# Reordering the opening of a two-layer decoder kernel: one table first, four PSUM banks for the input's transposes, dummies in a bank of their own, the first weights in four transfers

## The chip, the cores and the metric

One core of a Trainium2 chip runs the whole kernel. The metric is the device time of one execution in microseconds (us), the median of several runs.

## The reference

A decoder trunk of two layers on 256 tokens of width 1024, float32. Each layer is a mixer and a mixture of experts, each with a residual and a layer norm. The opening concerns the first lines alone: the input's layer norm and the mixer's one combined projection.

```python
h = layer_norm(x, ln_in_g, ln_in_b)
for l in range(2):
    # inside mixer_block: split_cols(h @ w_in[l], IN_SPLITS) feeds three attention mixers and three gates
    mix = mixer_block(h, l, w_in[l], ...)
    h = layer_norm(DEEPNORM_ALPHA * h + mix, ln1_g[l], ln1_b[l])
    ffn = moe_ffn(h, router_w, router_b, moe_w1[l], moe_w3[l], moe_w2[l])
    h = layer_norm(DEEPNORM_ALPHA * h + ffn, ln2_g[l], ln2_b[l])
```

## The kernel before

**Precision.** A projection is computed from operands split in two: a high half rounded to fp32r and a low half that holds the rest. One product is three matmuls (high by high, low by high, high by low). ScalarE casts the high half of a weight block (L370, or L949 for the first one), VectorE subtracts to get the low half (L371, L950). Each block is 128 partitions by 2048 columns, 1 MB, split 1024 columns at a time.

**Weights** come through a ring of SBUF slots (`Stream`, L81 to L136). A load is issued on SP as soon as a slot is free, in a fixed order: "q" 0 and 1 (the query columns), "kv" 0 and 1, "ng", and so on. The block ("q", 0) is loaded in two transfers (L98), every other in one.

**The opening** (L186 to L217, L1681 to L1699). ScalarE's queue issues the identity (`idf`, from `consts`) and then the per-column constants (`pc`). SP issues x, one transfer for each half of 128 tokens, and then the weights. While the data comes, TensorE runs three dummy matmuls on a tile of ones (`junk`, L1688), into a buffer of the same PSUM pool that the transposes use. `raw_T` (L287) transposes x, eight column tiles by two token halves (L291). A tile of 128 x 256 takes one of four PSUM buffers. `raw_split` (L294) multiplies it by the norm's gain: ScalarE writes the high half (`z`, L297), VectorE the low half (L298), and then the buffer is free for the tile four places on.

**The raw products.** The query projection does not wait for the layer norm. Block ("q", 0) (L964) and block ("q", 1) (L375 to L377, from `z`) are multiplied with the raw, transposed x, 48 matmuls each, and corrected afterwards with the tokens' scale and shift (L977 to L980). The first block is split in two halves of four tiles: the first by L949 and L950 (`gl`), the second by `split` (L370, L371). The load of the norm's gain and bias rows (`gb`, L216) is issued on ScalarE's queue behind the cast of L949.

**The norm.** `norm` (L922) computes statistics of each token half (L310), aggregates them (L254), takes a reciprocal root by three steps of Newton's method (L235 to L242), the shift (L260), and normalizes x in place: VectorE does the first 512 columns (L271), ScalarE the others (L267). TensorE transposes the result (L319), ScalarE applies gain and bias (L337), VectorE splits it (L338, L339), and the "kv" projection is the first product with the normalized input (`acc<-hi,whi`, L375). Layer 1 does the same with values that the experts' stage left, through the same lines, except that x is there already transposed and its statistics are read in PSUM (L935).

**What sets the order.** The kernel is written in one order. A scheduler turns it into one instruction stream for each engine, by a list of ready instructions, priorities and its own estimates of time. `tc.issue_after(i)` holds an instruction behind `i` on the same engine. Each engine runs its stream in that order. The same program gives each DMA one of eight completion counters in turn.

Of the kernel before, what the change touches and what calls it, by code (L numbers as in the profile page):

```python
# [9 lines left out]
F32 = mybir.dt.float32  # L10
# [4 lines left out]
ALU = mybir.AluOpType  # L15
AX = mybir.AxisListType
PSUM = bass.MemoryType.PSUM

L = 2
P = 128  # L20
D = 1024
S = 256
KD = D // P
# [13 lines left out]
LOANS = (6, 7)  # L37
NW = 16
NW2 = 24
NW0 = 3  # L40
NS = NA + 3 + NB + 2 + NC + 1
EARLY = set()
DOWN = [[], [0], [1], [2, 3], [], [4], [5], [6, 7]]
# [8 lines left out]
CB_SEL = CB_IOTA + 64  # L52
CB_LOW = CB_SEL + 2
CB_TRI = CB_LOW + 16
CB_ID = CB_TRI + P
CB_N = CB_ID + 3 * P

PC_LN = 0
PC_QG = 80
# [3 lines left out]
PC_N = PC_POS + 64  # L63
# [6 lines left out]
def trunk(ctx, tc, x, consts, pcol, rowv, gb, wfm, wng, wdv, wmla, wcmp, wcmp2, wu, wbr, wout, rw, mw1, mw3, mw2, out):  # L70
    import numpy as np
    nc = tc.nc
    slopes = [float(v) for v in _slopes(np)]
    V, A, T, G = nc.vector, nc.scalar, nc.tensor, nc.gpsimd

    cst = ctx.enter_context(tc.tile_pool(name="cst", bufs=1))
# [4 lines left out]
    class Stream:  # L81
# [6 lines left out]
        def load(self, slots, item):  # L88
            slot = slots.pop(0)
            key, src, n = item  # L90
            t = slot[0].tile([P, 2048], F32, name="wt", tag=slot[1])
            eng = nc.sync
            if key[1:] == ("w2", 15, 1):
                for c in (0, 256):
                    d, v = [a.rearrange("p (b c) -> p b c", c=512)[:, :, c:c + 256] for a in (t, src)]
                    eng.dma_start(d, v)
            else:
                parts = 2 if key[1:] == ("q", 0) else 1  # L98
                for c in range(0, n, n // parts):
                    eng.dma_start(t[:, c:c + n // parts], src[:, c:c + n // parts])  # L100
            self.live[key] = (t, slot, slots)
# [83 lines left out]

    rt = hp.tile([P, 2, D], F32, name="r")  # L186
    idb = cst.tile([P, 3 * P], F32R, name="idb")
    pc = cst.tile([P, PC_N], F32, name="pc")
    start = ExitStack()
    gi = start.enter_context(tc.tile_pool(name="gi", bufs=1, reuse_waits="tile"))  # L190
    ident = gi.tile([P, P], F32, name="idf")
    nc.scalar.dma_start(ident, consts[:, CB_ID + P:CB_ID + 2 * P])
    nc.scalar.dma_start(pc, pcol)
    for t in range(2):
        nc.sync.dma_start(rt[:, t], x[t * P:(t + 1) * P, :])
    ST.pump()
# [66 lines left out]
    def ln_norm2(r, sts, src=None):  # L263
        mr, nbs, _ = ln_mr2(sts)
        for t in range(2):
            d = r[:, t, 512:1024]
            A.activation(d, d if src is None else src[t][1], AF.Identity, bias=nbs[t], scale=mr[t][1])  # L267
        for q in range(2):
            for t in range(2):
                d = r[:, t, 256 * q:256 * q + 256]  # L270
                i = V.tensor_scalar(d, d if src is None else src[t][0][:, 256 * q:256 * q + 256], mr[t][0], mr[t][1],  # L271
                                    op0=ALU.subtract, op1=ALU.mult)
        return [rs for mu, rs in mr], nbs, i.ins
# [10 lines left out]
            z += [(zt[:, k, 0], zt[:, k, 1]) for k in range(n)]  # L284
        return z

    def raw_T(r, i, ks, z, psp):  # L287
        for k in ks:
            ps = psp.tile([P, S], F32, name="pt")
            for t in range(2):  # L290
                T.transpose(ps[:, t * P:(t + 1) * P], r[:, t, k * P:(k + 1) * P], ident)  # L291
            raw_split(ps, i, k, z)

    def raw_split(ps, i, k, z):  # L294
        g = ln_cols(i, k)[0]
        hi, lo = [v[:, 0:S] for v in z[k]]
        X0["z", k] = A.activation(hi, ps, AF.Copy, scale=g).ins  # L297
        V.scalar_tensor_tensor(lo, ps, g, hi.bitcast(F32), op0=ALU.mult, op1=ALU.subtract)  # L298

    def raw_fix(rs, nbs, psp, bc):  # L300
        ps = psp.tile([P, 2, S], F32, name="s")
# [5 lines left out]
    def ln_stats(r, t):  # L307
        st = sm.tile([P, 2, 6], F32, name="lnst")
        for c in range(2):
            V.bn_stats(st[:, c], r[:, t, c * 512:(c + 1) * 512])  # L310
        return st
# [31 lines left out]
    def mixer(l, res, z, zf):  # L343
# [578 lines left out]
        def norm():  # L922
            r, i = res, 2 * l
            pool, tag = ST.take()
            if zf is None:
                rs, nbs, X["norm"] = ln_norm2(r, [ln_stats(r, t) for t in range(2)])
            else:
                zt = [[p.tile([P, 512], F32, name=n) for c in range(2)] for p, n in ((pO, "o"), (pS, "s"))]
                sts = [sm.tile([P, 2, 6], F32, name="lnst") for t in range(2)]
                for c in range(2):  # L930
                    for t in range(2):
                        for k in range(4):
                            with tc.issue_after(X["raw", 0, 0]):
                                T.transpose(zt[t][c][:, k * P:k * P + P], zf[:, 4 * c + k, t * P:t * P + P], ident)
                        V.bn_stats(sts[t][:, c], zt[t][c])  # L935
                rs, nbs, X["norm"] = ln_norm2(r, sts, zt)
            bc = pool.tile([P, 2048], F32, name="bc", tag=tag)
            psps = [(pT, "pt"), (pT, "pt"), (pO, "o"), (pO, "o"), (pS, "s")]
            xT[:] = ln_split_T(r, i, X["evq"], psps, *(ST.take() if zf is None else X0["zf"]))
            with tc.issue_after(X["evq"]):  # L940
                raw_fix(rs, nbs, pS, bc)
            return bc
# [2 lines left out]
        add_tm("ng", xT, 280, ev2)  # L945
        w = wtile("q", 0, KD, 256)
        gl = mg.tile([P, 2, 4, 256], F32R, name="gl", tag="gt0")
        with tc.issue_after(X0["z", 1 if "yh" in X0 else 3]):
            i = A.copy(gl[:, 0], w[:, 0:4])  # L949
        V.tensor_sub(gl[:, 1], w[:, 0:4], gl[:, 0].bitcast(F32))  # L950
        with tc.issue_after(i.ins):
            w0 = [(gl[:, 0], gl[:, 1]), split(w[:, 4:8], [P, 4, 256], mb, OHL[1][1])]
        with tc.issue_after(i.ins):
            for c in fq[2:4]:
# [724 lines left out]
        return r, Z.get("z"), Z.get("zf")  # L1679

    with start as st:  # L1681
        pi = st.enter_context(tc.tile_pool(name="pi", bufs=4, space=PSUM))
        A.activation(one, one, AF.Identity)
        junk = gi.tile([P, 4 * P], F32, name="junk")
        V.memset(junk, 1.0)
        pj = pi.tile([P, S], F32, name="pt")
        for _ in range(NW0):
            T.matmul(pj, junk[:, 0:P], junk[:, 0:S], start=True, stop=True)  # L1688
        trf = gi.tile([P, P], F32, name="trf")
        zero = gi.tile([P, P], F32, name="zero")  # L1690
        G.memset(zero, 0.0)
        for j, v in enumerate((zero, ident, zero)):
            G.tensor_copy(idb[:, j * P:j * P + P], v)
        nc.sync.dma_start(trf, consts[:, CB_TRI:CB_ID])
        V.tensor_copy(tri, trf)
        z = raw_tiles(0)
        raw_T(rt, 0, range(KD), z, pi)
        ident = idb[:, P:2 * P].bitcast(F32)

    zf = None  # L1700
# [8 lines left out]
def _consts(np):  # L1709
# [21 lines left out]
    ang = np.arange(256, dtype=f)[:, None] * freqs[None, :]  # L1731
    c[:, CB_COS:CB_COS + 32] = np.cos(ang).astype(f).reshape(2, P, 16).transpose(1, 0, 2).reshape(P, 32)
    c[:, CB_SIN:CB_SIN + 32] = np.sin(ang).astype(f).reshape(2, P, 16).transpose(1, 0, 2).reshape(P, 32)
    c[:, CB_ID + P:CB_ID + 2 * P] = np.eye(P, dtype=f)
    c[:, CB_TRI:CB_TRI + P] = (np.arange(P)[:, None] < np.arange(P)[None, :])
    c[:, CB_IOTA:CB_IOTA + 64] = np.arange(1, 65)[None, :]
    c[:, CB_LOW:CB_LOW + 16] = (np.arange(4)[:, None] > np.arange(4)[None, :]).astype(f).reshape(1, 16)
# [4 lines left out]
def _pack(np, inp):  # L1742
# [61 lines left out]
    for l in range(L):  # L1804
        for n in ("cmp_pos_k", "cmp_pos_v"):
            pcs.append(a[n][l].reshape(16, 2, 64).transpose(1, 2, 0).reshape(P, 16))
    pcol = np.concatenate(pcs, 1)
    rowv = np.concatenate([a["router_b"]] + [a["diff_lambda"][l].reshape(-1) for l in range(L)])
    return {
        "x": a["x"].reshape(S, D), "consts": _consts(np), "pcol": pcol, "rowv": rowv, "gb": gb, "wfm": wfm, "wng": wng, "wdv": wdv,  # L1810
# [20 lines left out]
```

## Time and profile before

| | us |
|---|---|
| median of 3 runs | 1046.31 |
| the runs | 1044.56 to 1046.35 |
| the profiled execution | 1044.16 |
| its span, first to last instruction | 1042.5 |

The profiled execution is one execution by itself. Its span is a little shorter than its time, which also holds what lies before the first instruction and after the last. PE is TensorE's matmul part, PEld its weight load, DVE is VectorE, ACT ScalarE, POOL GpSimd; a q behind an engine's name (ACTq, SPq) is its queue, where it issues DMAs. Busy times say what an engine did, waits what it stood for: an idle stretch is put down to what ended it. The times in a timeline count from the first instruction.

### The profile page before, as it was taken

To read this page: it belongs to the slowest core of one execution; us is meant where nothing else is said; L and a number is where in the kernel's file an instruction comes from. 1 tells how busy PE (TensorE), PEld (TensorE's weight loads), DVE (VectorE), ACT (ScalarE), POOL (GpSimd) and SP (SyncE) were. 2 spreads that over 40 slices of the span, in tenths; PEclk is the share of its full clock that TensorE was granted. 3 is DMA by queue.
4 is the path that set the end of the run, shared out by engine and by line. 5 is a ranking of instruction groups with operands and counts; after the bars stand their busy time and mean duration, and the time that the engine had idled before them with its cause. 6 is when DMAs were issued, how large, how long until landed. Compare 5 with 4: busy or idle time off the path is not lost. (4 is left out here: it accounts for less than half of the span.)

```text
span 1042.5 us, 16792 instructions
## 1 busy us (share of the span) xinstructions
PE 1005.7 (96%) x6498; PEld 707.3 (68%) x6498; DVE 533.7 (51%) x1493; ACT 423.7 (41%) x991; POOL 31.7 (3%) x46
## 2 busy tenths in 40 slices
PE   8999999999989999999899999999999999989994
PEld 7888888999864344433597888799998544424332
DVE  7755778785772121211395558777777422102315
ACT  6564677564432121211455547755553221101110
POOL 0300000000000000000001001000000000000001
PEclk8999999999999999999999999999999999999998
DMA  9664334548867999999955544345497789999993
GB/s 358 250 243 137 138 122 164 182 141 345 321 258 302 422 420 420 420 421 420 389 182 215 188 152 155 130 146 177 158 374 300 290 321 422 421 418 421 420 421 133
DMA packets 45543, 294.88 MB, mean 283 GB/s; under 512 B 5136, under 2 KB 7952, under 8 KB 11792
## 3 DMA queue, kind: packets, MB, share of 16 engines
q1 hardware_dynamic: 44880, 291.51, 71.3%
q10 hardware_dynamic: 576, 2.24, 0.5%
q8 instruction: 51, 0.84, 0.3%
q14 instruction: 36, 0.29, 0.1%
HBM read 292.68 MB, written 1.05 MB: 282 GB/s over the span
## 5 line engine op out<-in xcount | busy, mean ns | idle before, releaser
L1557 PE MATMUL pt<-wt,xe 128*64 128x512 f32 x1024 | 226.3, 598 | 5.3 <-DVEq L1453 4.7
L371 DVE TENSOR_TENSOR wlo<-wt,whi 128x1024 fp32r<-128x1024 f32 (+4 forms) x146 | 167.4, 1148 | 81.9 <-ACT whi L370 75.7
L370 ACT CAST whi<-wt 128x1024 fp32r<-128x1024 f32 (+4 forms) x146 | 143.8, 987 | 147.1 <-PE acc L376 103.5
L1557 PEld LDWEIGHTS pt<-wt,xe 128*64 128x64 f32 x1024 | 72.9, 138 | 143.9 <-issue 133.7
L375 PE MATMUL acc<-hi,whi 128*128 128x256 f32 x576 | 165.4, 289 | 1.7 <-ACT whi L370 0.8
L377 PE MATMUL acc<-hi,wlo 128*128 128x256 f32 x576 | 164.0, 286 | 0.8 <-DVE wlo L371 0.8
L376 PE MATMUL acc<-lo,whi 128*128 128x256 f32 x576 | 162.3, 282 | 0.0
L1600 PE MATMUL pt<-wt,gT 128*64 128x512 f32 (+1 forms) x544 | 113.9, 568 | 0.0
L375 PEld LDWEIGHTS acc<-hi,whi 128*128 128x128 f32 x576 | 108.1, 188 | 7.9 <-issue 3.9
L377 PEld LDWEIGHTS acc<-hi,wlo 128*128 128x128 f32 x576 | 108.3, 188 | 4.2 <-DVE wlo L371 2.1
L376 PEld LDWEIGHTS acc<-lo,whi 128*128 128x128 f32 x576 | 108.7, 189 | 0.3 <-DVE lo L339 0.2
L1609 ACT CAST yh<-pt 128x512 fp32r<-128x512 f32 (+1 forms) x34 | 19.1, 560 | 184.2 <-PE pt L1600 184.2
L1600 PEld LDWEIGHTS pt<-wt,gT 128*64 128x64 f32 x544 | 38.7, 137 | 70.6 <-issue 65.8
L1610 DVE TENSOR_TENSOR yl<-pt,yh 128x512 fp32r<-128x512 f32 (+1 forms) x34 | 22.4, 659 | 106.0 <-ACT yh L1609 106.0
L1568 DVE SCALAR_TENSOR_TENSOR g<-g,pt 128x512 f32<-128x512 f32 x16 | 11.0, 686 | 126.6 <-ACT g L1567 126.6
L1567 ACT ACTIVATE g<-pt 128x512 f32<-128x512 f32 x16 | 9.6, 597 | 120.4 <-PE pt L1557 120.4
L375 PE MATMUL acc<-ob,whi 128*128 128x256 f32 x192 | 56.8, 296 | 1.1 <-DVE gt L892 0.8
L376 PE MATMUL acc<-ob,whi 128*128 128x256 f32 x192 | 54.2, 282 | 0.0
L377 PE MATMUL acc<-ob,wlo 128*128 128x256 f32 x192 | 54.2, 284 | 0.0
L1569 DVE SCALAR_TENSOR_TENSOR g<-g,wsl,pt 128x512 f32<-128x512 f32 x16 | 11.9, 746 | 69.0 <-PE pt L1557 69.0
L659 DVE COPY ts<-pt 128x384 f32<-128x384 f32 x56 | 30.5, 551 | 30.7 <-PE pt L628 30.6
L1382 ACT ACTIVATE xe<-pt,pc 128x128 f32<-128x128 f32 x60 | 24.2, 453 | 53.3 <-PE pt L1324 51.6
(399 smaller groups left out, 1763.1 us busy)
## 6 DMA issues: line engine op xcount, KB each, us to landing
wt<-in_mw SPq DMA_DIRECT2D x190, 1024.0 KB, 16.8
wt<-in_wfm SPq DMA_DIRECT2D x38, 1024.0 KB, 4.9
wt<-in_wbr SPq DMA_DIRECT2D x12, 1024.0 KB, 4.8
wt<-in_wcmp SPq DMA_DIRECT2D x8, 1024.0 KB, 6.2
wt<-in_wout SPq DMA_DIRECT2D x8, 1024.0 KB, 8.1
wt<-in_wdv SPq DMA_DIRECT2D x4, 1024.0 KB, 6.2
wt<-in_wmla SPq DMA_DIRECT2D x4, 832.0 KB, 5.8
wt<-in_wng SPq DMA_DIRECT2D x4, 560.0 KB, 12.8
```

The source lines that it names most:

```text
L370: X["hi"] = A.copy(hi, src).ins
L371: X["lo"] = V.tensor_sub(lo, src, hi.bitcast(F32)).ins
L375: T.matmul(ps, a[0], b[0], start=start, stop=False)
L376: T.matmul(ps, a[0], b[1], start=False, stop=False)
L377: return T.matmul(ps, a[1], b[0], start=False, stop=stop)
L659: X["ts"] = V.tensor_copy(ts, pt).ins
L1382: A.activation(x[:, k], pj, AF.Identity, bias=bb, scale=g)
L1557: i = T.matmul(hh[64 * j:64 * j + 64], xe[p][:, 2 * h + k, j * CAP:(j + 1) * CAP], wt[:, c0:c0 + FF], start=(h == 0 and k == 0), stop=(h = ...
L1569: V.scalar_tensor_tensor(g, g, wsl[:, p:p + 1], h3, op0=ALU.mult, op1=ALU.mult)
L1600: i = T.matmul(v[64 * j:64 * j + 64], gT[:, 2 * h + f, 64 * j:64 * j + 64], w2t[:, c0 + ks[0] * P:c0 + ks[1] * P], start=(h == 0 and f == ...
L1609: X0["yh"] = A.copy(yh[:, d], v).ins
L1610: V.tensor_sub(yl[:, d], v, yh[:, d].bitcast(F32))
```

## The change

- The identity is put ahead of the per-column constants in one table (`pct`), loaded in one transfer on ScalarE's queue ahead of all else. It leaves `consts`.
- The block ("q", 0) of layer 0 comes in four transfers, that of layer 1 in two as before.
- The transposes of x go into four tiles of a whole PSUM bank, two column tiles in each. All of the first token half come first, then all of the second, in an order written out. ScalarE's eight high halves are chained one behind another.
- The dummies go into a bank of their own: four ahead of the transposes, and three behind them.
- The cast of the first half of the first block (`gl`) is done in two pieces, behind the second and the fourth tile of `z` in layer 0; the other half's cast follows the last tile there.
- In layer 0 VectorE's statistics of the second token half follow the last low half of `z`, and the aggregation and normalization follow the low halves of the second block.
- The cast of the triangular mask (`tri`) goes from VectorE to GpSimd.

```diff
-NW0 = 3
+NW0 = 4
+NW1 = 3
...
-                parts = 2 if key[1:] == ("q", 0) else 1
+                parts = (4 if key[0] == 0 else 2) if key[1:] == ("q", 0) else 1
...
-    pc = cst.tile([P, PC_N], F32, name="pc")
+    pct = cst.tile([P, P + PC_N], F32, name="pc")
+    ident, pc = pct[:, 0:P], pct[:, P:]
...
-    ident = gi.tile([P, P], F32, name="idf")
-    nc.scalar.dma_start(ident, consts[:, CB_ID + P:CB_ID + 2 * P])
-    nc.scalar.dma_start(pc, pcol)
+    nc.scalar.dma_start(pct, pcol)
...
-    def raw_T(r, i, ks, z, psp):
-        for k in ks:
-            ps = psp.tile([P, S], F32, name="pt")
-            for t in range(2):
-                T.transpose(ps[:, t * P:(t + 1) * P], r[:, t, k * P:(k + 1) * P], ident)
-            raw_split(ps, i, k, z)
+    def raw_T(r, i, z, psp, fill):
+        ps = [psp.tile([P, 2, S], F32, name="pt") for k in range(KD // 2)]
+        ps = [v[:, k] for k in range(2) for v in ps]
+        for t in range(2):
+            for k in range(KD):
+                with tc.issue_after(fill):
+                    fill = T.transpose(ps[k][:, t * P:(t + 1) * P], r[:, t, k * P:(k + 1) * P], ident).ins
+        for k in range(KD):
+            with tc.issue_after(X0["z", k - 1]) if k else nullcontext():
+                raw_split(ps[k], i, k, z)
+        return fill
...
-        V.scalar_tensor_tensor(lo, ps, g, hi.bitcast(F32), op0=ALU.mult, op1=ALU.subtract)
+        X0["zl", k] = V.scalar_tensor_tensor(lo, ps, g, hi.bitcast(F32), op0=ALU.mult, op1=ALU.subtract).ins
...
-                rs, nbs, X["norm"] = ln_norm2(r, [ln_stats(r, t) for t in range(2)])
+                sts = [ln_stats(r, 0)]
+                with tc.issue_after(X0["zl", 7]):
+                    sts.append(ln_stats(r, 1))
+                with tc.issue_after(X["lo"]):
+                    rs, nbs, X["norm"] = ln_norm2(r, sts)
...
-        with tc.issue_after(X0["z", 1 if "yh" in X0 else 3]):
-            i = A.copy(gl[:, 0], w[:, 0:4])
-        V.tensor_sub(gl[:, 1], w[:, 0:4], gl[:, 0].bitcast(F32))
-        with tc.issue_after(i.ins):
+        for n, k in enumerate((1, 1) if "yh" in X0 else (1, 3)):
+            v = slice(2 * n, 2 * n + 2)
+            with tc.issue_after(X0["z", k]):
+                i = A.copy(gl[:, 0, v], w[:, v])
+            V.tensor_sub(gl[:, 1, v], w[:, v], gl[:, 0, v].bitcast(F32))
+        with tc.issue_after(i.ins if zf is not None else X0["z", 7]):
             w0 = [(gl[:, 0], gl[:, 1]), split(w[:, 4:8], [P, 4, 256], mb, OHL[1][1])]
...
-        pi = st.enter_context(tc.tile_pool(name="pi", bufs=4, space=PSUM))
+        pi = st.enter_context(tc.tile_pool(name="pi", bufs=4, space=PSUM, reuse_waits="tile"))
...
-        pj = pi.tile([P, S], F32, name="pt")
-        for _ in range(NW0):
-            T.matmul(pj, junk[:, 0:P], junk[:, 0:S], start=True, stop=True)
+        pjp = st.enter_context(tc.tile_pool(name="pj", bufs=1, space=PSUM, reuse_waits="tile"))
+        pj = pjp.tile([P, S], F32, name="pj")
+
+        def fill(n):
+            for _ in range(n):
+                i = T.matmul(pj, junk[:, 0:P], junk[:, 0:S], start=True, stop=True)
+            return i.ins
+        warmed = fill(NW0)
...
-        V.tensor_copy(tri, trf)
+        G.tensor_copy(tri, trf)
         z = raw_tiles(0)
-        raw_T(rt, 0, range(KD), z, pi)
+        with tc.issue_after(raw_T(rt, 0, z, pi, warmed)):
+            X0["fill"] = fill(NW1)
```

## Rows read from the trace of the kernel before

**Rows 1.** The page's first line.
```profile
span 1042.5 us, 16792 instructions
```

**Rows 2.** Busy time by stretch: us, PE, PEld, DVE, ACT, POOL, granted clock, DMA share, GB/s.
```profile
6.00:8.60 2.60, 0.65 (x4) 0.42 (x4) 2.53 (x13) 1.57 (x4) 0.00 (x0) 1.00 0.86 285
8.97:15.70 6.73, 6.45 (x30) 5.89 (x29) 6.67 (x20) 5.56 (x8) 0.00 (x0) 0.50 1.02 432
...
20.00:1040.00 1020.00, 990.42 (x6425) 694.59 (x6424) 518.24 (x1446) 412.47 (x973) 30.50 (x38) 0.99 0.72 282
```

**Rows 3.** Waits of the whole kernel: us in total, times, longest us.
```profile
PE pt L1557 <- DVEq L1453: 4.7, 1, 4.7
PEld pt L1600 <- DMA wt<-in_mw: 2.0, 5, 0.8
```

**Rows 4.** Timeline of PE in the opening: start us, us, what, idle before.
```profile
1.71 2.93 PE L1688 MATMUL pt<-junk 128*128 128x256 f32 x6 [1.71 <-DVE junk L1685]
5.12 0.83 PE L291 MATMUL pt<-idf,r 128*128 128x128 f32 x4 [0.48 <-DMA idf<-in_consts]
6.37 0.65 PE L291 MATMUL pt<-idf,r 128*128 128x128 f32 x4 [0.42 <-DMA r<-in_x]
8.66 1.28 PE L291 MATMUL pt<-idf,r 128*128 128x128 f32 x4 [1.64 <-DVE z L298]
10.10 2.52 PE L964 MATMUL acc<-z,gl 128*128 128x258 f32 x10 [0.15 <-ACT gl L949]
...
18.00 1.12 PE L964 MATMUL acc<-z,wlo 128*128 128x258 f32 x8
...
27.92 0.28 PE L375 MATMUL acc<-hi,whi 128*128 128x256 f32 x1
```

**Rows 5.** Timeline of ScalarE and its queue in the opening.
```profile
6.74 1.57 ACT L297 ACTIVATE z<-pt,pc 128x256 fp32r<-128x256 f32 x4 [3.47 <-PE pt L291]
9.00 1.04 ACT L949 CAST gl<-wt 128x1024 fp32r<-128x1024 f32 x1 [0.70 <-DMA wt<-in_wfm]
10.29 0.34 ACTq L216 DMA_DIRECT2D gb<-in_gb  x1
10.67 0.47 ACT L297 ACTIVATE z<-pt,pc 128x256 fp32r<-128x256 f32 x1 [0.62 <-DMA wt<-in_wfm]
```

**Rows 6.** DMA issues of the first 40 us: KB each, median us to landing.
```profile
pc<-in_pcol ACTq DMA_DIRECT2D x1, 76.0 KB, 5.3
idf<-in_consts ACTq DMA_DIRECT2D x1, 64.0 KB, 4.2
```

**Rows 7.** Groups of VectorE from 4.8 to 29.7 us: busy us, mean ns, idle before.
```profile
L371 DVE TENSOR_TENSOR wlo<-wt,whi 128x1024 fp32r<-128x1024 f32 x7 | 8.6, 1222 | 2.6 <-ACT whi L370 2.5
...
L310 DVE BATCH_NORM_STATS2 lnst<-r 128x6 f32<-128x512 f32 x4 | 2.6, 682 | 3.2 <-DMA r<-in_x 3.2
```

**Rows 8.** Timelines of VectorE and PE in layer 1's norm.
```profile
528.86 0.32 DVE L254 BATCH_NORM_AGGREGATE lnmv<-lnst 128x2 f32<-128x12 f32 x2
529.33 1.22 DVE L371 TENSOR_TENSOR wlo<-wt,whi 128x1024 fp32r<-128x1024 f32 x1
533.13 0.99 DVE L271 TENSOR_SCALAR r<-s,lnmv,rqy 128x256 f32<-128x256 f32 x2
535.53 0.38 PE L319 MATMUL pt<-idb,r 128*128 128x128 f32 x2
538.23 0.50 PE L375 MATMUL acc<-hi,whi 128*128 128x256 f32 x2
```

**Rows 9.** The mask's readers: duration ns min, median, max, first and last start.
```profile
L1215 PEld LDWEIGHTS <-tri x2: 102/142/181, 294.7 to 300.5; 128*128 128x128 bf16 x2
```

**Rows 10.** Timeline of VectorE in the opening: a step of the norm and a low half.
```profile
15.07 0.21 DVE L240 SCALAR_TENSOR_TENSOR rqt<-rqy,rqh 128x1 f32<-128x1 f32 x1
15.20 1.22 DVE L371 TENSOR_TENSOR wlo<-wt,whi 128x1024 fp32r<-128x1024 f32 x1
```

**Rows 11.** Timeline of SP's queue.
```profile
9.00 0.33 SPq L200 DMA_DIRECT2D rb<-in_rowv  x1
12.77 0.33 SPq L1694 DMA_DIRECT2D trf<-in_consts  x1
```

More of the change, by code (lines that the diff above doesn't have):

```diff
@@ L54 @@
 CB_TRI = CB_LOW + 16
-CB_ID = CB_TRI + P
-CB_N = CB_ID + 3 * P
+CB_N = CB_TRI + P
 PC_LN = 0
@@ L1693, in trunk @@
             G.tensor_copy(idb[:, j * P:j * P + P], v)
-        nc.sync.dma_start(trf, consts[:, CB_TRI:CB_ID])
-        V.tensor_copy(tri, trf)
+        nc.sync.dma_start(trf, consts[:, CB_TRI:CB_N])
+        G.tensor_copy(tri, trf)
         z = raw_tiles(0)
-        raw_T(rt, 0, range(KD), z, pi)
+        with tc.issue_after(raw_T(rt, 0, z, pi, warmed)):
+            X0["fill"] = fill(NW1)
         ident = idb[:, P:2 * P].bitcast(F32)
@@ L1733, in _consts @@
     c[:, CB_SIN:CB_SIN + 32] = np.sin(ang).astype(f).reshape(2, P, 16).transpose(1, 0, 2).reshape(P, 32)
-    c[:, CB_ID + P:CB_ID + 2 * P] = np.eye(P, dtype=f)
     c[:, CB_TRI:CB_TRI + P] = (np.arange(P)[:, None] < np.arange(P)[None, :])
@@ L1806, in _pack @@
             pcs.append(a[n][l].reshape(16, 2, 64).transpose(1, 2, 0).reshape(P, 16))
-    pcol = np.concatenate(pcs, 1)
+    pcol = np.concatenate([np.eye(P, dtype=np.float32)] + pcs, 1)
     rowv = np.concatenate([a["router_b"]] + [a["diff_lambda"][l].reshape(-1) for l in range(L)])
```

## The prediction

> **What bounds the kernel now.** I read the page first, then TensorE's waits, then the first 30 us by engine. The profiled execution took 1044.16 us: a span of 1042.5 [rows 1] and 1.66 around it. Its median is 1046.31 us, so the profiled execution is 2.15 under the median; the sum below is made against the profiled one and the difference taken off the median. A measurement of this kernel can tell about 0.2% from no change, 2.1 us.
>
> After the opening TensorE is the bound: from 20 to 1040 us it is busy 990.42 of 1020 us [rows 2], its longest single wait is 4.7 us, at a branch that the change leaves alone, and a wait for expert weights is 0.8 us at most [rows 3]. So whatever TensorE reaches earlier in the opening should move all that follows by as much. In the opening the reader should see three things. TensorE idles from about 7.0 to 8.66 us, because only four input transposes have a PSUM buffer and the fifth waits for VectorE to empty one [rows 4]. Right behind that idle time, from 8.97 to 15.70 us, the granted clock is 0.50, the 1.2 GHz level; ahead of it it is 1.00, 2.4 GHz, and over the rest of the kernel 0.99 [rows 2]. In that stretch the first products (L964) come every 0.25 us (10 in 2.52), later every 0.13 (8 in 1.12) [rows 4]. And ScalarE, which makes the high halves, is stopped twice by data: the first half of the first weights is there at 9.00, and the fifth input tile waits until 10.67 behind the load of gb, which could itself be issued only at 10.29 [rows 5].
>
> The opening as a chain: the first product group (L964, 48 products) ends at 18.00 + 1.12 = 19.1, and the first product with the normalized input starts at 27.92 [rows 4]. These 8.8 us hold another 48 products of the raw input and the transposes of the normalized one.
>
> **The change part by part.**
> - One table. The identity landed 4.2 us after its issue, the per-column constants 5.3 after theirs [rows 6]; the first transpose started with the identity at 5.12 [rows 4]. The joint table has as many rows as either and is issued where the identity was, so I give it 4.2 to 5.3: landing 5.1 to 6.2. I take 5.3, near the identity, since the table too is first in its queue, beside the same transfer of x. The later end costs some 0.6 us at the far side.
> - Four dummies for three: six instructions took 2.93 us at half clock [rows 4], so eight take 3.9 and end at 5.6. Until 5.3 they cover the wait for the table, at most 0.3 us is paid, and x's second half arrives at 6.37 [rows 4] anyway: nothing.
> - Transposes. Four take 0.65 us [rows 4], so 0.16 each at most; eight of the first token half from 5.6, eight of the second from 6.4 to 6.9, all done by 8.2, where before the last ones stood among the products. A tile shares its bank with the one four places on, so ScalarE may have to wait for the fifth: first tile at 7.1, where it was 6.74 [rows 5].
> - Three dummies behind them: 1.5 us if the clock is up, until 9.7, 2.9 if it is down. They fill the place where TensorE idled.
> - First weights in quarters. Before, the halves were there at 9.00 and 10.29 (the gb load waits for the second, see below), 1.29 apart; the quarters then come at about 7.9 (half a half earlier than 9.00, and a bit, 285 GB/s flowing there [rows 2]), 9.0, 9.7 and 10.3. Two more issues on SP come ahead of the second block; its data queue behind 2.2 MB anyhow and stay hidden.
> - ScalarE's path, the one that I think ends last: 8 input tiles at 0.39 (four in 1.57), two quarter casts of 0.52 (1.04 for a half), the gb issue 0.35, the cast of the other half 1.04 [rows 5]: 5.6 us. From 7.1, with about 0.2 of waiting for the first quarter, this ends at 12.9. The gb load moves with the casts; more on that in the rivals. The first 24 products (2.9 us at full clock, from 9.7) are over by 12.6, hidden under it. The other 24 end at 15.9. Gain against 19.1: 3.2 us.
> - VectorE's order. The statistics of the second token half now follow the last input tile, and the normalization follows the low halves of the second block. By 12.3 the eight low tiles are done, one right behind each tile of ScalarE's. Then two statistics of 0.68 and three low halves of 1.22 at most [rows 7]: the normalization begins near 17.1 (they overlap at their ends), where before it was strung through all of this. What then remains is seen in layer 1, whose order is already the new one: from the aggregation at 528.86 to the first product with the normalized input at 538.23 are 9.4 us, with one low half (529.33) inside [rows 8]. There the values were ready at 534.1 and TensorE turned to them at 535.53, 1.4 us later, being full. So the path needs 8.0 to 9.4 us: that product starts between 25.1 and 26.5.
> - TensorE's own path gives 15.9 + 8.8 = 24.7.
> - The mask cast on GpSimd: one short cast fewer on VectorE. The mask is first read at 294.7 us [rows 9]. If it were late by many us nothing would wait; what queues behind it on GpSimd are memsets for the attention stage, and what covers that is the same distance. Nothing.
> - Layer 1's first cast in two pieces: nothing, two instructions' overhead on engines with idle time there, and the price below 0.1 us.
>
> The sum: the later of 24.7 and 25.1 to 26.5. I take 25.5, near the lower end, because most of the 1.4 us in layer 1 is TensorE being occupied and not the path. Against 27.92 that is **2.4 us gained**: 1041.8 for the profiled execution, 1046.3 - 2.4 = 1043.9 for the median. By the upper end it is 1.4, by TensorE alone 3.2.
>
> **The rivals.**
> 1. *The normalization is the new bound.* Before, the scheduler put low halves between the steps of the normalization's chain (15.07 and 15.20 [rows 10]). If both low halves of the third block get in, 1.2 us more than in layer 1, the first normalized product starts at 26.3 to 26.7: gain 1.2 to 1.6, time 1044.9. For it: one got in in layer 1 [rows 8]. Against: their casts on ScalarE are late themselves.
> 2. *The clock falls all the same.* If TensorE's short runs don't hold it, the first 24 products take 6.0 us from 9.7, the other 24 then end near 18.7 at full clock, and TensorE's own path gains 0.4; with a rise midway, 1.5. I take 0.9, time 1045.4. For: between 9.7 and 12.9 TensorE waits for quarters and tiles. Against: the gap of 1.6 us that went ahead of the fall is filled.
> 3. *Slower: gb's load stops ScalarE.* The DMA issues wait for the transfer eight places earlier: rb, the 13th, went at 9.00 with the 5th (the first half), the mask, the 15th, at 12.77 with the 7th (the second block) [rows 11], and between them gb, the 14th, at 10.29 [rows 5]. After the change one transfer more stands ahead of gb, and the second block is now the 8th. As the 15th gb waits for the last quarter (10.3, in my sum); if the mask's load goes first it is the 16th and waits for the second block, 12.8. ScalarE then makes the fifth tile at 13.1 instead of 10.67, the low tiles end at 15.2, the normalization starts at 20.0 and the first normalized product stands at 28.0 to 29.4, with rival 1 on top 30.6. TensorE, with nothing to do from 12.6 to 15.7, would likely lose its clock as well; its second 24 products at 0.25 end at 21.7 and its own path at 30.5. That is slower by 0.1 to 2.7; I take 2.2 of the two together, time 1048.5. It decides from the point where gb's issue is later than about 12.3. Against it: in the order of before gb came ahead of the mask.
> 4. *The start doesn't reach the end.* In the expert stages TensorE waits for weights a little [rows 3]. If that stream has no reserve the waits grow by what is gained: 1046.3. Against: the loads are issued as slots come free and so move with TensorE.
> 5. *The quarters come late.* Each is only 256 KB. If each paid a cost of its own, the first product group would lack its last weights. By the halves, 1.29 us apart for 0.5 MB, nothing of the sort is seen: they flow. Paying 1 us more for each of the two added transfers, the cast of the second half starts near 12.4 and the gain is 1.9, time 1044.4. The Trainium skill, "DMA: Bandwidth & Descriptors", "Rules for kernel authors", speaks against the split: at least 1 MiB per DMA for the most bandwidth. Its fit for one transfer, a fixed 2.0 us and bytes at 436 GB/s (fitted for another issuing engine), would make four in a row 4 us dearer than two, an estimate of about 1 us gained in all; the trace's halves disagree, since they overlap.
> 6. *More than the sum:* all paths short, 3.2 to 4.2 us, time 1042.6.
>
> **How the numbers follow.** Forecast 0.46, rival 1 0.16, rival 2 0.10, rival 3 0.12, rival 4 0.04, rival 5 0.04, rival 6 0.08. Faster by over 0.2%: nearly all of the forecast (0.45) and rival 6: 0.53. Within 0.2%: rivals 1, 2, 4, 5, the mild third of rival 3 (0.04) and the forecast's rest: 0.39. Slower: the rest of rival 3, 0.08. Predicted is the likeliest, 1043.9. The limit of 0.2%, 1044.2, runs close to it. The range leaves out the slower cases and the far end of rival 6: 1041.8 to 1046.4.
>
> **What would show it.** Right: no idle TensorE between the transposes and the products, the granted clock at 1.00 from 8.97 to 15.70, all transposes ahead of 8.5, first product group over near 16, first normalized product near 25.5, and the same rows behind it, moved by as much. Wrong: a stretch at 0.50 after 9 us; gb issued after 12 us; ScalarE waiting for PSUM; low halves standing inside the normalization; waits for expert weights longer than the 0.8 us of now.

## The result and the profile after

The changed kernel takes 1052.44 us in the median of 5 runs (1050.12 to 1058.87) against 1046.22 for the kernel before, in 5 runs beside them: a ratio of 1.0086, 95% interval 1.0065 to 1.0107, which is that of the means, 1054.4 to 1045.5: the runs scatter over 9 us, those of before over 2. It is slower. The prediction, 1043.9 with a range of 1041.8 to 1046.4 and 0.08 for slower, was wrong. The profiled execution took 1058.68 us, one of the two longest, so its delays are those of a long run.

The page's first line, and TensorE's longest waits (us in total, times, longest us):

```profile
span 1056.7 us, 16815 instructions
```

```profile
PE pt L1567 <- PEq L1463: 6.1, 1, 6.1
PE pt L1567 <- DVEq L1463: 4.6, 1, 4.6
PE acc L974 <- ACT whi L374: 3.1, 1, 3.1
PE pt L1567 <- DVE mxf L1409: 1.8, 1, 1.8
```

The 4.6 us were there before [rows 3], at the branch of layer 1 (926.64 us before). The other three are new, and they lie in three places: in the opening, at layer 0's overflow branch near 420 us, and in layer 1 near 828 us.

**The opening.** TensorE's timeline:

```profile
1.71 3.77 PE L1701 MATMUL pj<-junk 128*128 128x256 f32 x8 [1.71 <-DVE junk L1695]
5.34 2.21 PE L292 MATMUL pt<-pc,r 128*128 128x128 f32 x16
7.39 1.46 PE L1701 MATMUL pj<-junk 128*128 128x256 f32 x6
8.95 3.13 PE L974 MATMUL acc<-z,gl 128*128 128x258 f32 x24
15.18 3.50 PE L974 MATMUL acc<-z,whi 128*128 128x258 f32 x16 [3.09 <-ACT whi L374]
18.47 1.36 PE L974 MATMUL acc<-z,wlo 128*128 128x258 f32 x8
...
27.01 0.74 PE L323 MATMUL pt<-idb,r 128*128 128x128 f32 x4 [0.79 <-DVE lnnb L259]
...
30.19 0.49 PE L379 MATMUL acc<-hi,whi 128*128 128x256 f32 x2
```

Up to 12.1 us all goes as planned: transposes without a gap, the first 24 products at full speed, where before they were strung out at half clock [rows 4]. Then TensorE idles 3.09 us. The first normalized product starts at 30.19, where it was 27.92 [rows 4]. ScalarE's timeline, with its queue, says why:

```profile
7.26 0.84 ACT L301 ACTIVATE z<-pt,pc 128x256 fp32r<-128x256 f32 x2 [4.48 <-PE pt L292]
7.99 0.62 ACT L959 CAST gl<-wt 128x512 fp32r<-128x512 f32 x1
8.50 0.85 ACT L301 ACTIVATE z<-pt,pc 128x256 fp32r<-128x256 f32 x2
9.22 0.63 ACT L959 CAST gl<-wt 128x512 fp32r<-128x512 f32 x1
12.24 0.33 ACTq L215 DMA_DIRECT2D gb<-in_gb  x1
12.62 1.57 ACT L301 ACTIVATE z<-pt,pc 128x256 fp32r<-128x256 f32 x4 [2.77 <-DMA wt<-in_wfm]
```

The quarters are there in time: neither cast of a quarter waits for one. But gb's issue stands on ScalarE's queue behind the second cast, can go out only at 12.24, and holds the other four input tiles for 2.77 us. SP's queue shows what got ahead of it: the mask's load, which went at 12.77 before [rows 11].

```profile
9.75 0.33 SPq L1709 DMA_DIRECT2D trf<-in_consts  x1
```

The clock, by stretch (us, PE, PEld, DVE, ACT, POOL, granted clock, DMA share, GB/s):

```profile
12.00:14.00 2.00, 0.09 (x1) 0.00 (x0) 0.87 (x3) 1.38 (x4) 0.00 (x0) 1.00 1.01 426
14.00:16.00 2.00, 0.82 (x5) 0.82 (x6) 2.00 (x6) 2.00 (x4) 0.00 (x0) 0.90 1.01 428
16.00:18.00 2.00, 2.00 (x11) 2.00 (x11) 2.00 (x2) 1.97 (x3) 0.00 (x0) 0.50 1.00 414
18.00:20.00 2.00, 1.83 (x12) 1.62 (x10) 2.00 (x5) 1.29 (x2) 0.00 (x0) 0.75 1.01 415
```

It is at 2.4 GHz until the idle time and falls to 1.2 behind it, so the second 24 products pay too (16 in 3.50 us). VectorE adds to it. Its norm chain, from the aggregation to the first shift, takes from 19.30 to 26.39, with two low halves in one place of it and one more in another:

```profile
19.30 0.27 DVE L253 BATCH_NORM_AGGREGATE lnmv<-lnst 128x2 f32<-128x12 f32 x2
19.49 2.30 DVE L375 TENSOR_TENSOR wlo<-wt,whi 128x1024 fp32r<-128x1024 f32 x2
...
24.34 1.22 DVE L375 TENSOR_TENSOR wlo<-wt,whi 128x1024 fp32r<-128x1024 f32 x1 [1.71 <-ACT whi L374]
...
26.39 0.15 DVE L259 SCALAR_TENSOR_TENSOR lnnb<-lnmv,rqy 128x1 f32<-128x1 f32 x1
```

**Behind the opening.** By the timelines' starts of the same instructions, TensorE is 3.0 us late at 300 us, 10.5 at 430, 11.2 at 808 and 14.4 at the end. The two jumps are these (TensorE's timeline, first expert product of each layer, each time first the kernel before and then the changed one):

```profile
412.72 12.67 PE L1557 MATMUL pt<-wt,xe 128*64 128x512 f32 x58 [0.48 <-PEq L1453]
```

```profile
421.32 5.12 PE L1567 MATMUL pt<-wt,xe 128*64 128x512 f32 x14 [6.05 <-PEq L1463]
```

```profile
815.21 1.94 PE L1557 MATMUL pt<-wt,xe 128*64 128x512 f32 x8 [0.15 <-DVE xe L1384]
```

```profile
828.02 3.58 PE L1567 MATMUL pt<-wt,xe 128*64 128x512 f32 x8 [1.79 <-DVE mxf L1409]
```

Line 1463 tests whether an expert has more tokens than its slots; when none has, TensorE branches past the code for that case. Before, the first product behind it waited 0.48 us for TensorE's own sequencer; now 6.05. In the stretch after it, 418 to 423 us, the granted clock is 0.54. At 828 the product waits for `mxf`, the maximum of the expert counts. In the compiled program the tiles of pool `pO` have traded PSUM banks 0 and 1 in layer 1: the counts now lie in bank 0, which is also the first bank of the expert products' pool, and must be read before it is free. The source does not say so anywhere, and no view of the profile shows it; e2_bank and e4_before_bank below test it.

### The profile page after: what moved, and what is told of

Read it like the earlier page. It is cut to its first block, busy times and chain, and to the rows that moved or that the text cites. A ratio compares the mean times of both kernels' runs of the same rounds, so it can differ in the third digit from the quotient of the medians.

```text
span 1056.7 us, 16815 instructions
## 1 busy us (share of the span) xinstructions
PE 1011.7 (96%) x6506; PEld 709.4 (67%) x6506; DVE 535.3 (51%) x1494; ACT 424.0 (40%) x993; POOL 31.8 (3%) x47
## 5 line engine op out<-in xcount | busy, mean ns | idle before, releaser
L1567 PE MATMUL pt<-wt,xe 128*64 128x512 f32 x1024 | 229.5, 605 | 12.5 <-PEq L1463 6.1
L1619 ACT CAST yh<-pt 128x512 fp32r<-128x512 f32 (+1 forms) x34 | 19.1, 561 | 184.2 <-PE pt L1610 184.2
## 6 DMA issues: line engine op xcount, KB each, us to landing
wt<-in_mw SPq DMA_DIRECT2D x190, 1024.0 KB, 15.9
```

The source lines that it names most:

```text
L1567: i = T.matmul(hh[64 * j:64 * j + 64], xe[p][:, 2 * h + k, j * CAP:(j + 1) * CAP], wt[:, c0:c0 + FF], start=(h == 0 and k == 0), stop=(h = ...
L1619: X0["yh"] = A.copy(yh[:, d], v).ins
```

## The experiments

The runs were made in three sets, each with the kernel before beside it (4 to 12 runs of a kernel, 14 to 30 of the kernel before). The ratios are of means. "Delay" is that of the same TensorE instruction against the profiled execution of the kernel before, in us.

| run | median us | ratio to before (95%) | delay at 300 | at 430 | at 808 | end |
|---|---|---|---|---|---|---|
| e1_gb | 1054.67 | 1.0093 (1.0078 to 1.0108) | -0.1 | 7.4 | 6.7 | 7.8 |
| e2_bank | 1055.23 | 1.0104 (1.0089 to 1.0119) | 3.5 | 6.7 | 6.1 | 6.6 |
| e3_gb_bank | 1053.34 | 1.0076 (1.0063 to 1.0090) | -0.3 | 6.9 | 7.4 | 9.2 |
| e4_before_bank | 1048.06 | 1.0026 (1.0017 to 1.0036) | 0.5 | 0.4 | 0.5 | 1.8 |
| e5_pad20 | 1055.43 | 1.0073 (1.0047 to 1.0099) | 1.4 | 8.5 | 9.8 | 11.2 |
| e6_pad6 | 1045.07 | 0.9994 (0.9984 to 1.0005) | -0.3 | -0.3 | -0.2 | -0.2 |
| e7_short | 1045.58 | 1.0003 (0.9990 to 1.0015) | 2.0 | 1.5 | 1.4 | 1.5 |
| e8_norm | 1045.93 | 0.9998 (0.9987 to 1.0009) | -0.4 | -0.5 | 0.3 | 1.8 |
| e9_wide | 1049.65 | 1.0034 (1.0019 to 1.0049) | 2.1 | 1.9 | 2.7 | 5.6 |
| e10_wide_gb | 1047.63 | 1.0017 (1.0006 to 1.0028) | 0.1 | 0.1 | -0.5 | 3.8 |
| e11_wide_gb_bank | 1045.70 | 1.0002 (0.9994 to 1.0011) | 1.4 | 1.0 | 0.3 | 0.8 |
| e12_wide_norm | 1044.83 | 0.9995 (0.9986 to 1.0004) | -0.4 | -0.3 | -0.9 | -0.9 |

The delays are of one execution each, and hold steps of 1.1 to 1.4 us that no repair explains: near 298 us in e5_pad20, e7_short and e11_wide_gb_bank (at 285 us their delays are -0.2, 0.4 and -0.2), near 520 in the changed kernel, e3_gb_bank, e5_pad20, e8_norm and e9_wide, and near 810 in e3_gb_bank, e5_pad20, e8_norm and e10_wide_gb. At each of them the granted clock reads 0.50, where in the kernel before it reads 1.00, or 0.50 for half as long. Whether they belong to the kernel or to the execution is open, so a difference of some 1.5 us between two delays need not come from the edit.

**First set: gb's load and the bank.** Theory: gb's load makes the opening late, the bank costs the wait at 828 us. e1_gb moves the load behind the last input tile; e2_bank gives layer 1 one more tile of `pO` (with a product that nothing reads), so that the counts come to lie in bank 1 again; e3_gb_bank does both; e4_before_bank puts the extra tile into the kernel before, whose counts then move to bank 0.

```diff
-            gbt = load_gb(mh, 2 * l, "gt1", nc.scalar)
+            with tc.issue_after(i.ins if zf is not None else X0["z", 7]):
+                gbt = load_gb(mh, 2 * l, "gt1", nc.scalar)
...
+            if l == 1 and t == 1:
+                sk = pO.tile([P, 2, E], F32, name="o")
+                pe(lambda: T.matmul(sk[:, 0], tri, mkb, start=True, stop=True))
             rk = pO.tile([P, 2, E], F32, name="o")
```

> The changed kernel with one edit: gb's load on ScalarE's queue goes behind the eighth input tile and no longer behind the second quarter cast. Theory (the opening is lost to that issue's wait for the second weight block): ScalarE's fifth input tile near 10 us instead of 12.62, no granted clock of 0.50 in the opening, first product with the normalized input near 26 instead of 30.19, and the whole about 4 us faster than the changed kernel, 1048 us where no other stall comes. Rival (the quarters or the clock are what delays the opening): fifth tile near 10 us, but the first normalized product still at 29 or later, and the whole within 1 us of the changed kernel.

> The changed kernel with one more PSUM tile and a tiny matmul in layer 1's gating, which gives the expert counts the PSUM bank that they had before (1), where the change left them in bank 0, the first bank of the expert stage. Theory (a swap of two banks, not the opening, makes TensorE wait 1.8 us for the counts' maximum at the start of layer 1's experts, and run at 1.2 GHz behind it): that wait goes, and the milestone there is 3.3 us earlier than in the changed kernel; the whole near 1049, opening as in the changed kernel. Rival (the wait there follows from the shifted times): the wait stays, same time as the changed kernel.

> Both edits. Theory: the two costs add, 7 us faster than the changed kernel where that has no stall at the branch: about 1044 to 1045, at or a little under the kernel before. If one of them only moves the other: 3 to 4 us gained in all. If runs near 1051 to 1052 remain beside these, the stall at the overflow branch is a third cost, independent of both.

> The kernel before with the same extra tile, which there gives the counts bank 0. Theory of the bank: 3 us slower than before, 1049, with a wait of 1.8 us for the counts' maximum ahead of layer 1's first expert product and a granted clock of 0.50 behind it. Rival: no change, 1046. The stall at the branch is in neither.

The opening did what the theory said, save that the first normalized product came at 27.07 and not near 26. In e1_gb TensorE's timeline and the clock of the prediction's stretch read:

```profile
14.62 1.21 PE L975 MATMUL acc<-z,wlo 128*128 128x258 f32 x8
...
23.90 0.74 PE L323 MATMUL pt<-idb,r 128*128 128x128 f32 x4 [0.80 <-DVE lnnb L259]
```

```profile
8.97:15.70 6.73, 6.36 (x48) 5.87 (x48) 6.73 (x13) 6.21 (x11) 0.00 (x0) 1.00 1.03 433
```

The clock no longer falls, the first 48 products end at 15.83 (19.1 before), and the delay at 300 us goes from 3.0 to -0.1. So the load of gb cost 3 us there, and nearly nothing is gained without it. Its issue goes out at 12.26 in e1_gb, for 12.24: moved down the queue it holds nothing, but what it waits for comes no earlier. The bank did too, in the wait: it is gone in e2_bank, and e4_before_bank brings it to the kernel before, and 0.26% with it. Its delay steps from 0.5 to 2.3 us there, without the half clock that was expected behind it (1.00 from 817 to 825 us); in the changed kernel, where the clock fell to 0.50, the step is 3.3.

```profile
PE pt L1560 <- DVE mxf L1402: 1.8, 1, 1.8
```

But the times did not follow: with both repaired, e3_gb_bank is still 0.76% slow. What remains is the branch: its wait was 5.9 us in e1_gb, 2.1 in e2_bank, 6.2 in e3_gb_bank, and 0.4 in e4_before_bank. It differs from kernel to kernel and hides what the other two are worth.

**Second set: the branch.** The instruction queue q8, which by the times of its fetches is TensorE's, gave a theory. In the ten microseconds from TensorE's arrival at the branch it fetches one block before, two after (DMA queues by stretch: packets, MB, share of 16 engines; first the kernel before from 412 to 422 us, then the changed one from 415 to 425):

```profile
q8 instruction: 1, 0.02, 0.7%
```

```profile
q8 instruction: 2, 0.03, 1.3%
```

Narrower stretches put the changed kernel's two fetches near 418.4 and 424.4 us, on either side of the restart at 421.3. The Trainium skill, "Runtime: NRT & Kernel Launch", "Instruction fetch mechanics", describes this: instructions are fetched one block after another, and a taken branch to a place that is not yet on chip stops the engine until its block has come. It gives no price. The traces agree: in each of the five kernels that stall (the changed one, the first three here and e5_pad20) the first expert product starts 1.8 to 1.9 us after the first of the two blocks has come, at 419.49 us in the changed kernel. In four of them that fetch begins 3.0 to 3.5 us after TensorE starts to wait; in e2_bank it had begun 0.8 us before, and the wait is the short one, 2.1 us. If so, the stall hangs on where the branch stands in TensorE's stream, and the changed kernel's stream is four dummy products longer there. e5_pad20 and e6_pad6 add 20 and 6 unused weight loads at the head of TensorE's stream to the kernel before; the order of its other instructions stays. e7_short is e3_gb_bank with fewer dummies (NW0 = 2, NW1 = 1). e8_norm also moves the norm up, to see what the opening could give.

```diff
         raw_T(rt, 0, range(KD), z, pi)
+        for _ in range(20):
+            nc.tensor.ldweights(ones)
```

```diff
-                with tc.issue_after(X["lo"]):
+                with tc.issue_after(X0["zl", 7]):
                     rs, nbs, X["norm"] = ln_norm2(r, sts)
...
-            A.activation(d, d if src is None else src[t][1], AF.Identity, bias=nbs[t], scale=mr[t][1])
+            X0["an"] = A.activation(d, d if src is None else src[t][1], AF.Identity, bias=nbs[t], scale=mr[t][1]).ins
...
-            fq[3].h = fq[3].prep(pool=mb, tags=OHL[1][1])
+            with tc.issue_after(X0["an"]) if zf is None else nullcontext():
+                fq[3].h = fq[3].prep(pool=mb, tags=OHL[1][1])
```

> The kernel before with twenty extra weight loads (of ones, used by nothing) at the head of TensorE's instructions; the order of everything else is the kernel before's. Theory P (the 6 us stall at layer 0's overflow branch belongs to the place of the branch in TensorE's instruction stream: its landing comes into a block of instructions that has not been fetched): the stall appears here too, a wait of 2 to 6.3 us put down to TensorE's own sequencer ahead of the first expert product (0.5 us in the kernel before), a fetch on the instruction queue that TensorE waits for and the next one within 7 us of it, and with the half clock behind it 3 to 8 us more at the end: 1048 to 1053. Rival Q (the stall comes with the changed opening, its order or its lateness, and not with the stream's length): no stall, 0.5 us, the time within 1 us of the kernel before.

> The same with six extra weight loads. Theory P: a shift of six instructions need not bring the landing over the edge of a block; if it does not, no stall and a time within 1 us of the kernel before; if it does, as with twenty. A third reading R (any change of the stream's length brings the stall) wants the stall here as well, 2 to 6.3 us. Rival Q: no stall.

> The changed kernel with gb's load behind the last of the eight raw tiles, the counts in their old bank, and two dummies ahead of the transposes and one behind them instead of four and three, so that TensorE's instruction stream up to the branch is four dummy products shorter, about as long as the kernel before's. Theory P: the stall is gone (0.6 us or less put down to the sequencer), and with it 6 to 7 us against the run with both repairs and seven dummies: 1045.5 to 1047.5, and at the branch no more behind the kernel before than at 300 us (0 +- 0.5 us). Rival Q: the stall stays at 5.9 to 6.2 and the time at 1053.

> The previous kernel, and the first normalization moved up: its steps on VectorE no longer wait for the low half of the last weight tile, and ScalarE's half of the normalization goes ahead of the cast of kv's second weight tile. Theory (with gb out of the way, the normalization chain is what bounds the opening): the wait of 0.8 us of the first normalized transposes goes, they begin at 22.9 or earlier, and the first normalized product starts at 25.0 to 26.3 instead of 27.1: 0.8 to 2 us less at 300 us and 1044 to 1046 at the end. Rival: the cast that now waits makes kv's products wait instead, the opening ends no earlier, and the time is the previous kernel's within 0.5 us.

Twenty weight loads, 0.99 us together, put off the dummies by 0.39 us and nothing behind the wait for the identity (transposes at 5.13, for 5.12 before). They cost the kernel before 0.73%; six cost nothing. The median, 1055.43, is above the 1048 to 1053 of theory P; three of the unexplained steps lie in this trace. The wait in e5_pad20, and then in e6_pad6:

```profile
PE pt L1557 <- PEq L1453: 6.5, 1, 6.5
```

```profile
PE pt L1557 <- PEq L1453: 0.4, 1, 0.4
```

q8 shows two packets in the first (413 to 423 us) and one in the second. In e7_short the wait is 0.4 us and the time is that of the kernel before. The opening of e5_pad20 is not late (-0.2 us at 285), and those of e7_short and e9_wide are, without a stall. So the place in the stream decides, which excludes rival Q, and not any lengthening brings the stall, which excludes reading R. All fourteen kernels agree: counted in the traces, the nine without the stall have 0 to 6 TensorE instructions more ahead of that product than the kernel before, the changed kernel and the three repairs that keep its dummies 17, e5_pad20 20. That an edge of a block lies between 6 and 17 is an inference from this count, q8 and the page; the edge itself was not located.

e8_norm gained in the opening, but later than forecast: the first normalized transposes at 23.28 (22.9 or earlier), without the wait, the first normalized product at 26.82 (25.0 to 26.3), 0.9 us ahead of e7_short at 285 us. Its time is that of e7_short. In its trace that gain goes in two stretches of half clock near 520 and 810 us, so the times show nothing gained, and why is open. Fewer dummies also had a side effect, in both runs: TensorE stood idle for 1.5 to 1.8 us ahead of the transposes, which then took 3.67 us for 2.21 in the changed kernel.

```profile
5.29 3.67 PE L292 MATMUL pt<-pc,r 128*128 128x128 f32 x16 [1.50 <-DMA pc<-in_pcol]
```

**Third set: one repair after another, without the stall.** All four have two dummies of 512 columns ahead of the transposes and one behind, so the same busy time ahead of them in four dummy products fewer overall. e9_wide is the changed kernel with that alone; e10_wide_gb, e11_wide_gb_bank and e12_wide_norm add gb's place, the bank, and the norm's order.

```diff
-NW0 = 4
-NW1 = 3
+NW0 = 2
+NW1 = 1
...
-        pj = pjp.tile([P, S], F32, name="pj")
+        pj = pjp.tile([P, 2 * S], F32, name="pj")
...
-                i = T.matmul(pj, junk[:, 0:P], junk[:, 0:S], start=True, stop=True)
+                i = T.matmul(pj, junk[:, 0:P], junk, start=True, stop=True)
```

> The changed kernel with its dummies made of fewer, wider products (two of 512 columns ahead of the transposes for four of 256, one of 512 behind them for three of 256), so that TensorE's stream up to the branch is four products shorter at nearly the same busy time; gb's load and the counts' bank stay as the change left them. If the three causes found so far (gb's load, the branch, the counts' bank) are separate and add up: the stall goes (0.6 us or less), the transposes keep their 2.2 us, the delay is 3.0 us at 300 us and grows by 1.7 to 2.9 us at the first expert product of layer 1, and the time is 1049 to 1052, 3.5 to 6 over the kernel before. Rival (the causes hide one another; without the stall the rest is absorbed): within 1.5 us of the kernel before.

> The same, and gb's load behind the last of the eight raw tiles. If the causes add up: 2.5 to 3.5 us less than the run without this, 1046 to 1049; the first normalized product at 27.1 and the delay at 300 us 0 +- 0.5 us; the counts' wait of 1.8 us remains. Rival: what the opening gains is lost in the branch over the experts, and the two runs are the same within 1 us.

> The same, and the counts of layer 1 in their old bank. If the causes add up: 1.7 to 2.9 us less than the run without this, 1044 to 1046, the kernel before's time within 1 us. Rival (something else of the change costs in layer 1): 1047 or more with no wait on the counts' maximum to be seen.

> The same, and the normalization moved up as in the earlier run, now with transposes at 2.2 us instead of 3.7. If that run gained nothing only because its transposes were slow: the first normalized transposes at 21.9 to 22.9, the first normalized product at 25.0 to 26.0, 1.5 to 2.5 us ahead of the kernel before at 300 us and 1043 to 1044.5 at the end, faster than both kernels. Rival (the branches over 60 to 300 us are paced by something that does not move with the opening): level with the run without this within 0.7 us.

Now the repairs can be read off one by one. From the changed kernel to e9_wide the ratio falls by 0.52% (the branch, about 5.4 us; the two stand in different sets, each beside its own kernel before), then by 0.17% (gb, 1.8 us), by 0.15% (the bank, 1.6 us) and by 0.07% (the norm's order, 0.7 us). The first three make 0.84% of the 0.86%: together they bring the time of the kernel before back, so the causes are complete. That they are separate and simply add is not shown, for steps in one order add up to the whole whatever they are. In the other order, gb and bank together gave 0.10% while the stall stood (1.0086 to 1.0076 in e3_gb_bank), and the branch then 0.74% (to 1.0002 in e11_wide_gb_bank), 7.7 us for 5.4; the intervals allow one price for both. Single sizes were off: gb's step is 2.0 us by the medians for 2.5 to 3.5, and 2.1 us of delay at 300 for 3.0; the transposes took 2.75 us in e9_wide and 2.50 in e11_wide_gb_bank for 2.2. Neighbouring intervals against the kernel before overlap. Compared with each other, the means fall by 2.0, 1.6 and 1.1 us, give or take 1.5, 1.0 and 0.8 (95%): the norm's order gains something, and little. e12_wide_norm is as fast as the kernel before and not measurably faster, against its theory's 1.5 to 2.5 us at 300 and 1043 to 1044.5 at the end. TensorE in its opening:

```profile
5.34 2.20 PE L292 MATMUL pt<-pc,r 128*128 128x128 f32 x16
...
22.31 0.38 PE L323 MATMUL pt<-idb,r 128*128 128x128 f32 x2
...
25.93 0.50 PE L379 MATMUL acc<-hi,whi 128*128 128x256 f32 x2 [0.82 <-DVE hi L342]
```

and its busy time in the next stretches, in the kernel before and in e12_wide_norm (us, PE, granted clock, DMA share, GB/s):

```profile
25.00:30.00 5.00, 5.00 (x45) 1.00 0.93 382
30.00:35.00 5.00, 5.00 (x44) 1.00 0.65 229
```

```profile
25.00:30.00 5.00, 4.09 (x33) 1.00 1.01 419
30.00:35.00 5.00, 4.83 (x41) 1.00 1.00 380
```

The first normalized product comes 2.0 us earlier than before, and then TensorE idles 0.91 + 0.17 us, waiting for VectorE's splits, where before it had work. Of the 1.1 us left at 45 us, 0.4 is left at 300. In between TensorE counts as busy and the order of its products is another; where the rest goes stays open.

This run shows one more thing. At layer 1's branch all the other kernels wait 4.5 to 4.7 us for VectorE's sequencer, the wait of rows 3; here it is 0.4. First the kernel before, then e12_wide_norm:

```profile
926.64 15.65 PE L1557 MATMUL pt<-wt,xe 128*64 128x512 f32 x64 [4.65 <-DVEq L1453]
```

```profile
921.47 13.95 PE L1572 MATMUL pt<-wt,xe 128*64 128x512 f32 x64 [0.36 <-PEq L1468]
994.90 1.94 PE L1572 MATMUL pt<-wt,xe 128*64 128x512 f32 x8 [0.53 <-DMA wt<-in_mw]
1009.71 1.94 PE L1615 MATMUL pt<-wt,gT 128*64 128x512 f32 x8 [0.55 <-DMA wt<-in_mw]
```

It then leads by 6.7 us, and from 995 to 1012 us loses it again in eight waits for expert weights, two of which are shown, with the DMA engines at 1.01 to 1.02; at the end it leads by 0.9, as it did at 920. So a gain as late as this does not reach the end: behind layer 1's branch the weights set it, and the wait there costs next to nothing. That it is the same stall, on VectorE's stream, is likely (VectorE's next instruction starts 5.7 us behind its own branch in the kernel before, 0.5 here) but not tested.

## Why the prediction was wrong

- **The step that failed first: "whatever TensorE reaches earlier in the opening should move all that follows by as much."** Nothing was put down for what lies behind 30 us. Of 9 us, about 7 arose there: 5.4 from the branch and 1.6 from the bank, by the third set. Neither is in a rival. A wait at that line, in layer 1, stood in the prediction [rows 3], as "a branch that the change leaves alone"; the change adds four dummies ahead of it in the same stream (17 TensorE instructions by the trace), and counted them at nothing because TensorE idled there. Their time is free, their number is not.
- **gb's load was the third rival, and happened as written.** The mask's load went first (9.75), gb was issued at 12.24 (12.8 was the sum), the fifth tile came at 12.62 (13.1), TensorE lost its clock, the first normalized product stood at 30.19 (28.0 to 29.4, or 30.6 with the first rival on top, which came too). Its chance, 0.12, rested on one argument against it. "In the order of before gb came ahead of the mask" was no argument, since the order is made anew for every edit. Its price, 2.2 us, was 3.0 at 300 us in the profiled execution and 2.1 in e9_wide.
- **The sum without gb's load.** ScalarE's path and the first 48 products were right: 15.83 in e1_gb for 15.9. The norm was not: 27.1 for 25.5, the first rival and 0.4 us beyond its upper end. Two low halves stand behind the aggregation, a third stands ahead of the chain's later steps and waits for its cast, which itself starts only when a product of the second block is done (20.15 in e1_gb, 23.26 in the changed kernel).
- **That a gain there would reach the end** failed also with the norm moved up (e12_wide_norm). Before, TensorE had raw products to do while the norm ran; once these are done earlier, it waits. Of the 2.0 us by which the first normalized product came earlier, about half came back as idle time up to 35. The fourth rival, that waits for expert weights grow by what is gained, is what happened to the 5.8 us gained at layer 1's branch. The 0.8 us by which this run led before had moved the loads along (862.61 for 863.37), as the prediction argued.
- **The small terms held.** The first transpose at 5.34 (the table was taken at 5.3), the four dummies 3.77 us (3.9), all transposes over at 7.55 (8.2), the first tile at 7.26 (7.1). The mask's cast ran at 23.42 on GpSimd, and nobody waited. The quarters came in time, in the changed kernel and in e1_gb: ScalarE waited for no quarter. The prediction's estimate of about 1 us less gain, from the fit for one transfer in the Trainium skill, "DMA: Bandwidth & Descriptors", "Anatomy of one DMA — SWDGE (gpsimd) path", is not borne out.
- **The clock.** That it would hold where TensorE is fed is right (1.00 up to 30 us in e1_gb), and that it falls behind an idle stretch of 3 us is too (0.50 from 16 to 18 us). That the first dummies run "at half clock" is right by their pace (0.47 us for an instruction ahead of the transposes, 0.24 behind them), but the granted clock reads 1.00 there.

## What to carry to other kernels

An instruction that is free in time still shifts everything behind it in its engine's stream. Where a kernel has a branch, look at the wait behind it and at the engine's instruction queue after every edit, and try the kernel with a few unused instructions more before judging an edit by its time. A DMA issue on a computing engine's queue can hold that engine for long, here 2.77 us: put it behind the work that the next engine needs. And before an idle stretch is counted as gain, ask what the engine will do in it when it gets there earlier.

## What the hardware showed that was not expected

- A skipped branch cost TensorE 0.4 to 0.5 us or 2.1 to 6.5, by the number of instructions ahead of it; 20 weight loads made the difference, 6 did not. In the changed kernel the delay grew by 7.5 us for 5.6 us more of waiting; the half clock behind it lies between the two.
- The same sixteen transposes took 2.20 to 2.75 us right behind dummies and 3.67 behind 1.5 us of idle time (273 ns each in the median in the changed kernel, 417 in e8_norm), although the granted clock reads 1.00 in both stretches: that column did not show it.
